# A transformer layer with window pooling on one core: sums in tiles of their own, pieces and high parts at other steps, a layer norm without GpSimd

## The chip, the core and the metric

The kernel runs on one core of a Trainium2 chip. A core has five engines with a queue each, worked off in program order: TensorE (PE, matrix products into PSUM banks of 128 x 512 floats), VectorE (DVE), ScalarE (ACT), GpSimd (POOL) and SyncE (SP, which here issues most transfers). They meet only at semaphores. The metric is the time of one execution on the device in microseconds (us).

## The reference

One layer for 1024 tokens of width 1024: a multi-scale pooling mixer, a layer norm, a SwiGLU channel mixer with hidden width 2816, and a second layer norm.

```python
x = layer_norm(ALPHA * x + g1 * ox, ln_g[i, 0], ln_b[i, 0])
x = layer_norm(ALPHA * x + g2 * swiglu(x * (1.0 + sc2) + sh2, ffn_w_in[i], ffn_w_out[i]),
               ln_g[i, 1], ln_b[i, 1])

def layer_norm(x, g, b):
    mu = jnp.mean(x, axis=-1, keepdims=True)
    var = jnp.mean(jnp.square(x - mu), axis=-1, keepdims=True)
    return (x - mu) * lax.rsqrt(var + LN_EPS) * g + b

def swiglu(h, w_in, w_out):
    gt, up = jnp.split(h @ w_in, 2, axis=-1)
    return (jax.nn.silu(gt) * up) @ w_out
```

## The kernel before

**Number format.** Every float32 operand of a product is split into a high part (a cast by ScalarE, `take_hi`, L267) and a low part (the rest, a subtraction by VectorE, `take_lo`, L270). A product is three matmuls: high x high, high x low, low x high.

**Fewer products.** Both matrix products of the channel mixer use a scheme of Strassen's kind: seven products of sums of blocks in place of eight products of blocks. The sums of the hidden activations a are made by VectorE (`a_sums`, `a_more_sums`) and stored in DRAM as a11, a2, s21 and s43. The sums of the output weights go to four DRAM tiles e1 to e4 and are made by 27 transfers that accumulate, the weight-sum pieces (`e_piece`, issued from GpSimd's queue); 18 of them stand in the loop over hidden blocks, nine in the last part.

**Three parts.** First come the modulation vectors, the pooling and the first layer norm; from 98 to 227 us the gate products; from 227 to 531 us the loop `period(f)` over 22 hidden blocks of 128. The last part, which the change is mostly about, is the output product: seven passes (`sub_pass(0)` to `sub_pass(6)`), one for each of the products p1 to p7, over 11 pairs of hidden blocks. A pair in a pass is a **step**; there are 77, numbered 0 to 76, 11 for each pass. One step is 12 matmuls: four row groups of 128 tokens, three matmuls each, into four banks. `heads` and `tails` group the first and last steps of a pass row group by row group, so that the row groups of a pass end apart; with `tails` 6 the last six steps are taken together.

**Order of the last part.** The Python code emits instructions in the order in which the engines' queues hold them. Ahead of each step `run_ahead` emits what is due: loads of step operands (`yraw`, two 128 x 512 transfers on SP's queue), splits (`yhi` by ScalarE, `ylo` by VectorE), pieces, and then the jobs that were given a time in steps: residual rows (`yrow`), products by the gate vector g2 (`scaled`), sums and the layer norm's steps. `LEAD` is how many steps the splits run ahead, growing over the passes, and `LOADS` how many more the loads do. Tiles of 128 x 1024 floats ("big") come from 45 places that are reused, the longest free first.

**Names.** u0 to u3, c0 to c3 and yv0, yv1 (two halves each) hold partial results of four row groups; `ps_x`, `ps_x2`, `ps_x3`, `ps_y`, `ps_y2` are the bank groups of the passes; mw holds a row's statistics. Rows 1 to 4 are finished in passes 5 and 6, rows 5, 6, 7 and 0 after pass 6. The mean and variance of a row come from `bn_stats` and `bn_aggr` on VectorE; for rows 5 to 0 the scaling is shared between ScalarE (`row_norm`), VectorE (`row_centre`, `row_scale`) and GpSimd (`by_line`).

Of the kernel before, what the change touches and what calls it, by code (L numbers as in the profile page):

```python
# [17 lines left out]
P = 128  # L18
# [201 lines left out]
def trunk_kernel(ctx: ExitStack, tc: tile.TileContext, x, c, mod_w, mod_b, ln_g, ln_b, ffn_w_in, ffn_w_out,  # L220
# [716 lines left out]
    def a_sums(j):  # L937

        x, y = tiles["a", 2 * j], tiles["a", 2 * j + 1]
        nc.vector.tensor_tensor(x[:, 1], y[:, 1], x[:, 1], ALU.subtract)  # L940
        nc.vector.scalar_tensor_tensor(x[:, 0], x[:, 1], -1.0, x[:, 0], ALU.mult, ALU.subtract)
        nc.sync.dma_start(s21_of[j], x)

    def a_more_sums(j):

        x, y = tiles["a", 2 * j], tiles["a", 2 * j + 1]
        for n in range(2):
            nc.vector.scalar_tensor_tensor(y[:, n], y[:, n], -1.0, x[:, 0], ALU.mult, ALU.subtract)

    def a_more_out(j):  # L950
        nc.sync.dma_start(s43_of[j], tiles["a", 2 * j + 1])
        done_with("big", f"a_{2 * j}", f"a_{2 * j + 1}")
# [101 lines left out]
    done = {"load": 0, "split": 0, "piece": IN_LOOP}  # L1054
# [6 lines left out]
    def step_split(n):  # L1061
        hi, lo = (big(f"y{q}{n}", F32R, (P, 2, HALF)) for q in ("hi", "lo"))
        split(hi, lo, raw.pop(n))
        operands[n] = hi, lo
        done_with("big", f"yraw{n}")

    def advance(kind, upto):
        while done[kind] < min(upto, STEPS):
            {"load": step_load, "split": step_split}[kind](done[kind])
# [61 lines left out]
    def row_stats(i, n, s):  # L1131
        if i not in st_of:
            st_of[i] = small(f"su{i}", (P, 3, 6), 8, "st")
        nc.vector.bn_stats(st_of[i][:, n, :], res[i][:, s])  # L1134

    def row_spread(i):
        mv = spread_of[i] = small(f"mw{i}", (P, 6), 8, "mv2")
        nc.vector.bn_aggr(mv[:, 0:2], st_of[i][:, : 3 if i == ORDER[1][3] else 2])

    def row_root(i):  # L1140
        mv = spread_of[i]
        nc.scalar.activation(mv[:, 2:3], mv[:, 1:2], ACT.Sqrt, bias=eps[:, 0:1])

    def row_factor(i):
        mv = spread_of[i]
        nc.vector.reciprocal(mv[:, 3:4], mv[:, 2:3])
        nc.vector.scalar_tensor_tensor(mv[:, 4:5], mv[:, 0:1], -1.0, mv[:, 3:4], ALU.mult, ALU.mult)

    def row_norm(i, s):
        mv, z = spread_of[i], res[i]  # L1150
        nc.scalar.activation(z[:, s], z[:, s], ACT.Identity, bias=mv[:, 4:5], scale=mv[:, 3:4])  # L1151

    def row_centre(i, s):
        z = res[i][:, s]
        nc.vector.scalar_tensor_tensor(z, z, spread_of[i][:, 0:1], lines["lg2"][:, s], ALU.subtract, ALU.mult)  # L1155

    def row_scale(i, s):
        z = res[i][:, s]
        nc.vector.scalar_tensor_tensor(z, z, spread_of[i][:, 3:4], lines["lb2"][:, s], ALU.mult, ALU.add)
# [5 lines left out]
    LEAD, LOADS = (3, 9), 4  # L1165
# [14 lines left out]
    def take_from(i, s, src):  # L1180
        z = res[i][:, s]
        nc.vector.tensor_tensor(z, z, src, ALU.subtract)
# [68 lines left out]
    with tc.manual_schedule():  # L1251
# [6 lines left out]
        advance("split", 3)  # L1258
# [22 lines left out]
        jobs = residual_jobs(0, 2.6, 2.2)  # L1281
# [6 lines left out]
        more = residual_jobs(1, 1.5 * PAIRS, 2.9)  # L1288
# [5 lines left out]
        jobs = [(1 + r, lambda r=r, i=i: add_into(i, first, c[r])) for r, i in enumerate(ORDER[0])]  # L1294
# [4 lines left out]
        jobs = [(r, lambda r=r, i=i: row_stats(i, 0, first)) for r, i in enumerate(ORDER[0])]  # L1299
        jobs += [(4, lambda: line_load("lg2", ln_g[1])), (4, lambda: line_load("lb2", ln_b[1]))]  # L1300
        more = [(t - PAIRS, job) for t, job in more if t >= PAIRS]
        for r, ps, _ in sub_pass(3, x_banks, True, 0, TAILS, jobs + more):
            v[r] = yv[r // 2][:, r % 2]
            nc.vector.tensor_tensor(v[r], ps, u[r], ALU.add)
        more = [(t - PAIRS, job) for t, job in more if t >= PAIRS]
        for r, ps, _ in sub_pass(4, x_banks, False, HEADS, TAILS, more):
            nc.vector.tensor_tensor(c[r], ps, u[r], ALU.add)
        y_banks = four("y2", "y")
        jobs, more = [], []
        for r, i in enumerate(ORDER[0]):  # L1310
            jobs.append((r / 2, lambda r=r: scaled(c[r], c[r], second)))
            jobs.append((r / 2 + 1, lambda r=r, i=i: take_from(i, second, c[r])))
            jobs.append((r / 2 + 2, lambda i=i: (row_stats(i, 1, second), row_spread(i))))
            jobs.append((r / 2 + 3, lambda i=i: row_root(i)))
            jobs.append((r / 2 + 4, lambda i=i: row_factor(i)))
            jobs.append((2 * r + 5, lambda i=i: row_centre(i, whole)))
            jobs.append((2 * r + 6, lambda i=i: row_scale(i, whole)))
            jobs.append((2 * r + 7, lambda i=i: row_out(i, whole)))
        more = [(t - PAIRS, f) for t, f in jobs if t >= PAIRS]
        for r, ps, _ in sub_pass(5, y_banks, True, 0, 1, jobs):  # L1320
            nc.vector.tensor_tensor(u[r], ps, u[r], ALU.add)
            nc.vector.tensor_tensor(v[r], ps, v[r], ALU.add)
        for r, i in enumerate(ORDER[1]):
# [50 lines left out]
```

## Time and profile before

| | |
|---|---|
| three timed runs | 764.58, 767.73, 768.26 us; median 767.73 |
| the profiled execution | 769.0 us, its span 767.2 us |
| VectorE busy | 565.1 us (74%) |
| ScalarE busy | 269.0 us (35%) |
| GpSimd busy | 172.2 us (22%) |
| transfers | 191.51 MB, mean 250 GB/s |

The span runs from the first to the last instruction of the profiled execution; what lies around it is 1.8 us. A row of a timeline has the start and the duration in us, the engine, the line, the operation, output <- inputs and a count; in brackets stands how long the engine was idle before and what released it. A row of the list of waits has the total in us, how many waits, and the longest. A row of the stages has the stretch, its length, the busy time of PE, PEld (weight loads), DVE, ACT and POOL with counts, the granted TensorE clock, the share of the DMA engines and GB/s. Back-to-back instructions of one engine overlap a little, so the distance of their starts is what one costs.

### The profile page before, as it was taken

How to read it: one execution, taken by the hardware profiler on the slowest of the kernel's cores; microseconds unless marked ns; L12 is line 12 of the kernel's file. 1: busy time of each engine (PE TensorE's matmuls, PEld its weight loads, DVE VectorE, ACT ScalarE, POOL GpSimd, SP SyncE). 2: the span in 40 equal slices, each digit the busy share in tenths (PEclk: the TensorE clock that was granted, in tenths of full speed). 3: DMA queues.
4: the chain of work that ended last, by engine and by line, in shares of the span. 5: the costliest groups of instructions: out<-in, count | busy, mean ns of one | idle time of the engine just before them, and what ended most of it. 6: DMA issues, size and time to landing. Idle time of an engine off the chain costs nothing.

```text
span 767.2 us, 9177 instructions
## 1 busy us (share of the span) xinstructions
PE 728.0 (95%) x3359; PEld 607.0 (79%) x3359; DVE 565.1 (74%) x686; ACT 269.0 (35%) x342; POOL 172.2 (22%) x132
## 2 busy tenths in 40 slices
PE   5988999999999999999999999998899999999991
PEld 5767988888887888888888888886678888888881
DVE  3598855517298787989889967864588759649997
ACT  0212873445982313113131131211467423334101
POOL 0000000020207554733725653511000000000015
PEclk8578999999999999999999999999999999999996
DMA  8998249585839698899999799699999858565202
GB/s 293 342 409 302 111 157 377 208 256 163 307 108 293 190 300 298 241 286 247 289 289 325 200 267 278 230 264 278 338 397 389 282 204 263 194 201 165 109 28 110
DMA packets 118019, 191.51 MB, mean 250 GB/s; under 512 B 7659, under 2 KB 66739, under 8 KB 117462
## 3 DMA queue, kind: packets, MB, share of 16 engines
q1 hardware_dynamic: 108326, 164.97, 62.5%
q0 software_dynamic: 9648, 25.95, 15.7%
q8 instruction: 26, 0.43, 0.2%
q14 instruction: 19, 0.16, 0.1%
HBM read 150.79 MB, written 66.06 MB: 283 GB/s over the span
## 4 chain that ended last, share of the span: by engine, by line
PE 74%; DVE 12%; DMA 10%; issue 2%; ACT 1%; POOL 0%; SPq 0%; POOLq 0%; DVEq 0%; ACTq 0%
PE ps_v L895 35%; PE ps_gate L761 15%; PE ps_x L1095 12%; DMA yraw<-in_ffn_w_out 5%; PE ps_y L1095 4%; DMA s21d<-a 2%; DMA mw<-in_mod_w 2%; PE ps_col L506 2%; DVE acc L491 2%; DVE ylo L270 2%; PE ps_pt L461 1%; DVE yrow L1155 1%; DVE su L1134 1%; PE ps_ox L262 1%; DVE yrow L1178 1%
## 5 line engine op out<-in xcount | busy, mean ns | idle before, releaser
L267 ACT CAST yhi<-yraw 128x1024 fp32r<-128x1024 f32 x77 | 79.6, 1053 | 88.6 <-PE ps_x L1095 21.5
L895 PE MATMUL ps_v<-t,w0h 128*128 128x512 f32 x352 | 109.3, 391 | 0.0
L761 PE MATMUL ps_gate<-h,wih 128*128 128x512 f32 x352 | 109.1, 391 | 0.0
L958 POOL TENSOR_TENSOR s<-raw,raw 128x512 f32<-128x512 f32 x22 | 30.9, 1405 | 323.6 <-DMA raw<-in_ffn_w_in 295.6
L270 DVE TENSOR_TENSOR ylo<-yraw,yhi 128x1024 fp32r<-128x1024 f32 x77 | 91.6, 1219 | 11.5 <-ACT yhi L267 8.2
L918 ACT ACTIVATE a<-a 128x512 f32<-128x512 f32 x22 | 13.9, 632 | 236.2 <-DVE a L917 236.2
L1095 PE MATMUL ps_x<-ylo,yhi 128*128 128x512 f32 (+1 forms) x231 | 88.6, 384 | 5.7 <-DVE ylo L270 5.7
L1095 PE MATMUL ps_x<-yhi 128*128 128x512 f32 (+1 forms) x231 | 88.4, 382 | 1.1 <-ACT u L1286 1.1
L1095 PE MATMUL ps_x<-yhi,ylo 128*128 128x512 f32 (+1 forms) x231 | 88.2, 382 | 0.0
L895 PEld LDWEIGHTS ps_v<-t,w0h 128*128 128x128 f32 x352 | 66.1, 188 | 14.5 <-issue 1.0
L761 PEld LDWEIGHTS ps_gate<-h,wih 128*128 128x128 f32 x352 | 65.7, 188 | 13.7 <-issue 0.5
L491 DVE SCALAR_TENSOR_TENSOR acc<-mw,s_col,acc 128x1024 f32<-128x1024 f32 x42 | 54.9, 1307 | 23.6 <-DMA mw<-in_mod_w 23.0
L895 PE MATMUL ps_v<-t,w0l 128*128 128x512 f32 x176 | 68.6, 390 | 1.8 <-DVE w0l L270 1.8
L761 PE MATMUL ps_gate<-h,wil 128*128 128x512 f32 x176 | 68.5, 389 | 0.0
L895 PE MATMUL ps_v<-t,ws 128*128 128x512 f32 x264 | 63.4, 389 | 0.0
L895 PEld LDWEIGHTS ps_v<-t,ws 128*128 128x128 f32 x264 | 49.6, 188 | 10.3
L1095 PEld LDWEIGHTS ps_x<-ylo,yhi 128*128 128x128 f32 x231 | 43.8, 190 | 15.7 <-DVE ylo L270 7.5
L1117 POOL TENSOR_TENSOR yrow<-yrow,line_lg 128x512 f32<-128x512 f32 (+2 forms) x4 | 5.8, 1460 | 224.0 <-ACT yrow L1151 224.0
L895 PE MATMUL ps_v<-h,w1h 128*128 128x512 f32 x176 | 54.2, 389 | 0.0
L895 PE MATMUL ps_v<-t,w1h 128*128 128x512 f32 x176 | 54.2, 389 | 0.0
L1095 PEld LDWEIGHTS ps_x<-yhi 128*128 128x128 f32 x231 | 43.8, 190 | 9.9 <-ACT u L1286 1.5
L1095 PEld LDWEIGHTS ps_x<-yhi,ylo 128*128 128x128 f32 x231 | 43.7, 189 | 8.1
(151 smaller groups left out, 1389.1 us busy)
## 6 DMA issues: line engine op xcount, KB each, us to landing
mw<-in_mod_w SPq DMA_DIRECT2D x48, 512.0 KB, 9.4
raw<-in_ffn_w_in SPq DMA_DIRECT2D x88, 256.0 KB, 6.6
ed<-in_ffn_w_out POOLq DMA_DIRECT2D x14, 1024.0 KB, 11.9
wi<-in_ffn_w_in SPq DMA_DIRECT2D x22, 512.0 KB, 6.0
yraw<-ed SPq DMA_DIRECT2D x44, 256.0 KB, 4.0
yraw<-in_ffn_w_out SPq DMA_DIRECT2D x33, 256.0 KB, 6.0
pd<-pk SPq DMA_DIRECT2D x11, 512.0 KB, 5.4
gd<-gk SPq DMA_DIRECT2D x11, 512.0 KB, 2.8
```

The source lines that it names most:

```text
L262: nc.tensor.matmul(ps, lh, rh, start=first, stop=False)
L267: nc.scalar.copy(hi, src)
L270: nc.vector.tensor_tensor(lo, src, hi.bitcast(F32), ALU.subtract)
L461: nc.tensor.matmul(pt_bank[half, ct][:, a:b], xr[ORDER[half][n]][:, ct * P : (ct + 1) * P], operand, start=n == 0, stop=False, skip_group_ ...
L491: nc.vector.scalar_tensor_tensor(acc, w, s_col[:, k : k + 1], acc, ALU.mult, ALU.add)
L506: nc.tensor.matmul(tiles["ps_col", j][:, n * WIDE : (n + 1) * WIDE], t[:, n * P : (n + 1) * P], by, start=first and n == 0, stop=last and ...
L761: nc.tensor.matmul(ps, x, y, start=k == n == 0, stop=k % 4 == 3 and n == 2, skip_group_check=k > 3)
L895: nc.tensor.matmul(ps, x, y, start=fresh and first, stop=last, skip_group_check=not fresh)
L918: nc.scalar.activation(a[:, 1], a[:, 1], ACT.Silu)
L958: nc.gpsimd.tensor_tensor(s, up1, up2, ALU.add)
L1095: nc.tensor.matmul(ps, s[x][:, r * P : (r + 1) * P], t[y][:, d], start=fresh and j == m == 0, stop=j == PAIRS - 1 and m == 2, skip_group_c ...
L1134: nc.vector.bn_stats(st_of[i][:, n, :], res[i][:, s])
```

## The change

**Sums.** `a_sums` and `a_more_sums` no longer overwrite the activations a; s21 and s43 get tiles of their own, and the activations' tiles come free earlier.

```diff
         x, y = tiles["a", 2 * j], tiles["a", 2 * j + 1]
-        nc.vector.tensor_tensor(x[:, 1], y[:, 1], x[:, 1], ALU.subtract)
-        nc.vector.scalar_tensor_tensor(x[:, 0], x[:, 1], -1.0, x[:, 0], ALU.mult, ALU.subtract)
-        nc.sync.dma_start(s21_of[j], x)
+        t = tiles["s21", j] = act_tile(f"s21_{j}")
+        nc.vector.tensor_tensor(t[:, 1], y[:, 1], x[:, 1], ALU.subtract)
+        nc.vector.scalar_tensor_tensor(t[:, 0], t[:, 1], -1.0, x[:, 0], ALU.mult, ALU.subtract)
+        nc.sync.dma_start(s21_of[j], t)
+        done_with("big", f"a_{2 * j}")
...
-        x, y = tiles["a", 2 * j], tiles["a", 2 * j + 1]
+        y, t = tiles["a", 2 * j + 1], act_tile(f"s43_{j}")
         for n in range(2):
-            nc.vector.scalar_tensor_tensor(y[:, n], y[:, n], -1.0, x[:, 0], ALU.mult, ALU.subtract)
+            nc.vector.scalar_tensor_tensor(t[:, n], y[:, n], -1.0, tiles["s21", j][:, 0], ALU.mult, ALU.subtract)
```

**Steps.** High and low parts are issued apart, the high part one step sooner; the lead grows to 11 steps, loads run three ahead of it; the nine last pieces get later step numbers.

```diff
         advance("load", int(step + ahead) + LOADS)
-        advance("split", int(step + ahead))
-        while done["piece"] < 3 * len(E_STEPS) and step >= 5 + 4.5 * (done["piece"] - IN_LOOP):
+        advance("hi", int(step + ahead) + 1)
+        advance("lo", int(step + ahead))
+        while done["piece"] < 3 * len(E_STEPS) and step >= 20 + 3 * (done["piece"] - IN_LOOP):
...
-    LEAD, LOADS = (3, 9), 4
+    LEAD, LOADS = (3, 11), 3
...
-        jobs = residual_jobs(0, 2.6, 2.2)
+        jobs = residual_jobs(0, 5, 2)
...
-        more = residual_jobs(1, 1.5 * PAIRS, 2.9)
+        more = residual_jobs(1, PAIRS, 2.1)
```

On SP's queue this moves the residual rows among the loads of pass 0. From the store of the last a11 on, before and after (xn is the stored residual row, `ffn_w_out` the output weights; yraw7 is the load of step 7):

```order
L933 DMA a11d10_86<-a_20_4098 128x512
L1059 DMA yraw7_4178<-a11d7_83 128x512
L1059 DMA yraw7_4178<-in_ffn_w_out 128x512
L1111 DMA yrow1_4185<-xn1_671 128x1024
L935 DMA a2d10_97<-a_21_4156 128x1024
L1059 DMA yraw8_4190<-a11d8_84 128x512
L1059 DMA yraw8_4190<-in_ffn_w_out 128x512
L942 DMA s21d10_108<-a_20_4098 128x1024
```

```order
L933 DMA a11d10_86<-a_20_4117 128x512
L1119 DMA yrow1_4204<-xn1_671 128x1024
L935 DMA a2d10_97<-a_21_4176 128x1024
L1063 DMA yraw7_4209<-a11d7_83 128x512
L1063 DMA yraw7_4209<-in_ffn_w_out 128x512
L943 DMA s21d10_108<-s21_10_4216 128x1024
L1063 DMA yraw8_4244<-a11d8_84 128x512
L1063 DMA yraw8_4244<-in_ffn_w_out 128x512
```

The first residual row and the store of a2 now pass ahead of step 7's loads; of the later residual rows the second moves from ahead of step 10 to behind it, and the third from ahead of step 14 to behind step 15. On ScalarE's queue, at the end of pass 0, where four copies take pass 0's result out of its banks into u0 to u3:

```order
L267 CAST yhi14_4387<-yraw14_4329 128x1024
L1286 COPY u0_4399<-ps_x_0_4174 128x512
L1286 COPY u1_4407<-ps_x_1_4175 128x512
L1286 COPY u2_4415<-ps_x_2_4176 128x512
L1286 COPY u3_4423<-ps_x_3_4177 128x512
L267 CAST yhi15_4428<-yraw15_4349 128x1024
```

```order
L267 CAST yhi14_4397<-yraw14_4353 128x1024
L267 CAST yhi15_4405<-yraw15_4373 128x1024
L1310 COPY u0_4415<-ps_x_0_4194 128x512
L1310 COPY u1_4423<-ps_x_1_4195 128x512
L1310 COPY u2_4431<-ps_x_2_4196 128x512
L1310 COPY u3_4439<-ps_x_3_4197 128x512
```

The high part of step 15 moved ahead of the copies. GpSimd's queue holds the nine pieces behind the sums of the last hidden block in both kernels, in the same order, and nothing between them.

**Banks.** Pass 6 (p7) goes on adding into the banks of pass 5 (p4), so that the sum of both comes out of one bank; it is taken row group by row group through all 11 steps, with four whole banks (before, the last row group was two halves). So the adds of pass 5's result into u, and u's product by g2, are gone from the end: u's own share of rows 5 to 0 is added in pass 3.

```diff
-        for r, ps, _ in sub_pass(5, y_banks, True, 0, 1, jobs):
-            nc.vector.tensor_tensor(u[r], ps, u[r], ALU.add)
+        for r, ps, _ in sub_pass(5, y_banks, True, 0, TAILS, jobs):
             nc.vector.tensor_tensor(v[r], ps, v[r], ALU.add)
...
-        for r, ps, d in sub_pass(6, x_banks, True, 0, 6, more):
+        for r, ps, d in sub_pass(6, y_banks, False, 0, PAIRS, more):
```

**Layer norm.** A row's sum comes from the accumulator outputs of the additions (`add_into`), its spread from a Square with accumulator on ScalarE; all rows but the last are then scaled by VectorE alone, one row behind. The last row keeps `bn_stats` and its division among three engines.

```diff
-    def row_spread(i):
-        mv = spread_of[i] = small(f"mw{i}", (P, 6), 8, "mv2")
-        nc.vector.bn_aggr(mv[:, 0:2], st_of[i][:, : 3 if i == ORDER[1][3] else 2])
+    def row_mean(i):
+        mv = row_sums(i)
+        nc.vector.tensor_scalar(mv[:, 2:3], mv[:, 0:1], mv[:, 1:2], -1.0 / D, ALU.add, ALU.mult)
+
+    def row_spread(i):
+        mv = row_sums(i)
+        nc.scalar.activation(scratch[0], res[i], ACT.Square, bias=mv[:, 2:3], accum_out=mv[:, 3:4])
+        nc.scalar.activation(mv[:, 4:5], mv[:, 3:4], ACT.Sqrt, bias=eps[:, 0:1], scale=1.0 / D)
...
-    def add_into(i, s, src):
+    def add_into(i, s, src, sign=1.0, sums=None):
         z = res[i][:, s]
-        nc.vector.tensor_tensor(z, z, src, ALU.add)
+        nc.vector.scalar_tensor_tensor(z, src, sign, z, ALU.mult, ALU.add,
+                                       **({} if sums is None else {"accum_out": row_sums(i)[:, sums : sums + 1]}))
...
+        def end_of_row(i):
+            row_factor(i)
+            row_centre(i, whole)
+            row_scale(i, whole)
+            row_out(i, whole)
```

On VectorE's queue, around the end of pass 5 (yv0 and yv1 take the result of pass 5 from the banks `ps_y2`; line_lg2 and line_lb2 are the norm's gain and shift), before and after:

```order
L270 TENSOR_TENSOR ylo74_5600<-yraw74_5520,yhi74_5599 128x1024
L1159 SCALAR_TENSOR_TENSOR yrow3_4315<-yrow3_4315,mw3_5453,line_lb2_5003 128x1024
L1321 TENSOR_TENSOR u0_4399<-ps_y2_0_5369,u0_4399 128x512
L1322 TENSOR_TENSOR yv0_4896<-ps_y2_0_5369,yv0_4896 128x512
L1321 TENSOR_TENSOR u1_4407<-ps_y2_1_5370,u1_4407 128x512
L1322 TENSOR_TENSOR yv0_4896<-ps_y2_1_5370,yv0_4896 128x512
L1321 TENSOR_TENSOR u2_4415<-ps_y2_2_5371,u2_4415 128x512
```

```order
L270 TENSOR_TENSOR ylo74_5596<-yraw74_5533,yhi74_5577 128x1024
L270 TENSOR_TENSOR ylo75_5613<-yraw75_5553,yhi75_5594 128x1024
L1160 SCALAR_TENSOR_TENSOR yrow3_4380<-yrow3_4380,mw3_4760,line_lg2_5120 128x1024
L270 TENSOR_TENSOR ylo76_5616<-yraw76_5574,yhi76_5611 128x1024
L1164 SCALAR_TENSOR_TENSOR yrow3_4380<-yrow3_4380,mw3_4760,line_lb2_5122 128x1024
L1348 TENSOR_TENSOR yv0_4934<-ps_y2_0_5408,yv0_4934 128x512
L1348 TENSOR_TENSOR yv0_4934<-ps_y2_1_5409,yv0_4934 128x512
```

The adds into u are gone, and the low parts of the last two steps and the third row's scaling now stand ahead of the first read of bank `ps_y2_0`.

More of the change, by code (lines that the diff above doesn't have):

```diff
@@ L1144, in row_factor, with row_sums @@
-    def row_factor(i):
[L1145 to L1151, printed above, removed]
+    def row_sums(i):
+        if i not in spread_of:
+            spread_of[i] = small(f"mw{i}", (P, 8), 8, "mv2")
+        return spread_of[i]
@@ L1328, in trunk_kernel @@
[L1328 to L1334 removed]
+            more.append((r, lambda r=r: scaled(v[r], v[r], second)))
```

130 lines of the change are left out of this document (72 added, 58 removed).

## The prediction

> **What bounds the kernel now.** I read the busy times first, then TensorE's waits, then the three engines round them in the last third.
>
> ```profile
> PE 728.0 (95%) x3359; PEld 607.0 (79%) x3359; DVE 565.1 (74%) x686; ACT 269.0 (35%) x342; POOL 172.2 (22%) x132
> PE ps_x L1095 <- DVE ylo L270: 5.7, 2, 3.3
> PE ps_x L1095 <- ACT u L1286: 1.1, 1, 1.1
> 600.50 29.92 PE ps_y L1095 x132
> 630.42 59.85 PE ps_x L1095 x264
> ```
>
> TensorE is busy 95% of the span, and the change leaves its work as it is: seven passes of 132 matmuls, 29.92 us each (0.227 us a matmul). So only what TensorE waits for, and what follows its last matmul, can go. After 380 us the list of waits has 6.8 us, all in the first pass (steps 0 to 10) or at its end; the chain runs without a gap from 570.28 through passes 1 to 4.
>
> ```profile
> 530.81 0.39 PE L1095 MATMUL ps_x<-yhi 128*128 128x512 f32 x1
> 533.66 0.50 PE L1095 MATMUL ps_x<-ylo,yhi 128*128 128x512 f32 x1 [2.47 <-DVE ylo L270]
> ...
> 537.51 0.39 PE L1095 MATMUL ps_x<-ylo,yhi 128*128 128x512 f32 x1
> ...
> 552.50 0.50 PE L1095 MATMUL ps_x<-ylo,yhi 128*128 128x512 f32 x1 [3.25 <-DVE ylo L270]
> ...
> 720.02 0.39 PE L1095 MATMUL ps_x<-yhi 128*128 128x512 f32 x1
> ...
> 750.35 0.28 PE L1095 MATMUL ps_x<-yhi,ylo 128*128 128x256 f32 x1
> ```
>
> Pass 0 starts at 530.81 and takes until 570.28, 9.5 us more than its work. Pass 6 starts at 720.02; TensorE ends at 750.63, and the span ends 16.6 us later. These are the two places.
>
> **Sums in tiles of their own.** VectorE's timeline shows what stands ahead of the low parts that TensorE waited for.
>
> ```profile
> 531.18 1.29 DVE L948 SCALAR_TENSOR_TENSOR a<-a,a 128x512 f32<-128x512 f32 x2 [6.19 <-DMA a2d<-a]
> 532.39 3.49 DVE L270 TENSOR_TENSOR ylo<-yraw,yhi 128x1024 fp32r<-128x1024 f32 x3
> ...
> 550.62 0.69 DVE L941 SCALAR_TENSOR_TENSOR a<-a 128x512 f32<-128x512 f32 x1 [4.99 <-DMA a11d<-a]
> 551.23 1.22 DVE L270 TENSOR_TENSOR ylo<-yraw,yhi 128x1024 fp32r<-128x1024 f32 x1
> ```
>
> Both sums overwrite a tile that is still being stored, and the low parts queue behind them. With other tiles both waits go. The arithmetic is the same, so the instructions cost what they cost. But what is late next? The loads:
>
> ```profile
> 500.00:545.00 45.00, 42.53 (x180) 34.44 (x179) 24.78 (x33) 9.56 (x11) 4.97 (x5) 0.96 1.09 265
> 545.00:600.00 55.00, 50.63 (x221) 40.99 (x220) 39.22 (x38) 32.06 (x33) 0.00 (x0) 1.00 1.05 392
> 546.60 1.05 ACT L267 CAST yhi<-yraw 128x1024 fp32r<-128x1024 f32 x1 [3.23 <-DMA yraw<-in_ffn_w_out]
> 548.83 1.05 ACT L267 CAST yhi<-yraw 128x1024 fp32r<-128x1024 f32 x1 [1.17 <-DMA yraw<-in_ffn_w_out]
> ...
> 568.70 1.05 ACT L267 CAST yhi<-yraw 128x1024 fp32r<-128x1024 f32 x1 [1.59 <-DMA yraw<-in_ffn_w_out]
> 569.65 2.04 ACT L1286 COPY u<-ps_x 128x512 f32<-128x512 f32 x4
> ```
>
> The last two columns of the stages are the DMA engines' share and GB/s: they are full from 500 to 600. ScalarE takes each high part when its load lands: step 5 at 546.60, step 6 at 548.83, step 14 at 568.70. A low part is ready 2.3 us after the landing (1.05 on ScalarE, 1.22 on VectorE). Without any wait TensorE would want step 5 at 530.81 + 5 x 2.72 = 544.4; it can have it at 548.9. So the first stall turns into waits for loads.
>
> From the landing of step 6 to that of step 14, 19.9 us, SP's queue has eight steps of two 128x512 loads (4 MB), three residual rows (1.5) and five stores (2.25): 7.75 MB, 0.39 MB/us. In its new order the first residual row and a store (1 MB) pass ahead of step 7, and the third residual row falls behind step 15. By bytes from 548.83, step 7 lands at 554.6, step 10 at 559.7, step 15 at 568.7 (again 7.75 MB). Step 10's low part, behind a residual row of 1.2 us on VectorE, is ready at 563.1. Steps 9 and 10 go together, 24 matmuls, and step 10 comes with the fourth: TensorE ends pass 0 at 563.1 - 0.9 + 5.4 = 567.6.
>
> **High parts a step sooner** adds nothing here, since high parts wait for landings; but it puts the high part of step 15 ahead of the four copies that free pass 0's banks. It is done at 568.7 + 1.05, the first copy about 0.5 later, and pass 1 starts at 570.3: as before. I take 0 for this place; bounds are a gain of 2.7 us (copies not held: 570.3 - 567.6) and, by TensorE's own rows, 7.5 us: the gaps of 2.47 and 3.25, and 1.8 for the slow clock behind the first (ten matmuls start from 533.66 to 537.51, nine steps of 0.43 instead of 0.227). A loss of 1.8 is possible too, if the clock falls in the same way behind the gap of 2.7 ahead of pass 1.
>
> The Trainium skill, "TensorE: Matmul & The Clock Gate", § Part 1: The HAM clock gate, lets the clock halve only after an idle window of about 3.4 us that runs free of the kernel. By it no gap here would be slowed and the sum stays at 0 for this place; by the rows behind 533.66 and 552.50, where 2.47 us were enough and 3.25 us were not, it can be 1.8 more.
>
> **Weight-sum pieces later.**
>
> ```profile
> 488.30 1.65 POOL L1043 DMA_DIRECT2D ed<-ed  x3
> ...
> 526.00 1.23 POOL L1043 DMA_DIRECT2D ed<-in_ffn_w_out  x1 [5.59 <-DMA ed<-in_ffn_w_out]
> ```
>
> The nine pieces of the loop over steps are all issued between 488 and 526, before step 0: they wait for each other and for nothing that TensorE does. GpSimd's queue has the same rows in the same order afterwards, so the later step number moves nothing: 0. If it did, pass 0's loads would have the 392 GB/s sooner.
>
> **Passes 1 to 4.** Products by g2 and sums move from pass 6 into pass 3, eight instructions of 0.6 us. VectorE has room:
>
> ```profile
> 600.00:690.00 90.00, 90.00 (x399) 74.55 (x398) 64.41 (x65) 33.23 (x32) 0.00 (x0) 1.00 0.68 220
> 690.00:720.00 30.00, 30.00 (x134) 24.84 (x133) 29.43 (x43) 13.42 (x16) 0.00 (x0) 1.00 0.47 158
> ```
>
> 4.8 us into 25.6 idle: 0.
>
> **Pass 5.** VectorE is full there (29.43 of 30). Now p7 is added into p4's banks, so pass 6's first matmul waits until VectorE has read bank 0 into yv0, and that read stands behind the low part of step 76 and the scaling of the third row.
>
> ```profile
> 690.30 0.69 DVE L1307 TENSOR_TENSOR c<-ps_x,u 128x512 f32<-128x512 f32 x1 [0.67 <-PE ps_x L1095]
> 690.90 1.22 DVE L270 TENSOR_TENSOR ylo<-yraw,yhi 128x1024 fp32r<-128x1024 f32 x1
> 692.04 1.29 DVE L1174 TENSOR_TENSOR c<-c,g 128x512 f32<-128x512 f32 x2
> 693.24 1.22 DVE L270 TENSOR_TENSOR ylo<-yraw,yhi 128x1024 fp32r<-128x1024 f32 x1
> 694.09 1.28 ACT L1142 ACT_TABLE_LOAD   x1
> 698.88 0.29 ACT L1142 ACTIVATE mw<-mw,eps 128x1 f32<-128x1 f32 x1 [3.51 <-DVE mw L1138]
> 706.35 1.28 DVE L1155 SCALAR_TENSOR_TENSOR yrow<-yrow,mw,line_lg 128x1024 f32<-128x1024 f32 x1
> L608 DVE DVE_READ_ACCUMULATOR x<-x,ps_ox x12: 80/83/84, 55.0 to 182.8; 128x1 f32 x12
> L629 ACT ACTIVATE sq<-x,mv x8: 1133/1136/1160, 79.8 to 194.6; 128x1024 f32<-128x1024 f32 x8
> L629 ACT ACTIVATION_READ_ACCUMULATOR sq<-x,mv x8: 183/186/194, 80.9 to 195.6; 128x1 f32 x8
> ```
>
> By the starts, a low part takes 1.14 us, half a row 0.60, a whole row 1.19; reading an accumulator 0.08. From 690.30: one sum 0.6, eleven low parts 12.5, four products 2.4, four sums with accumulator 2.7, six whole rows 7.1, eight small ones 0.8: 26.1. The bn_stats and bn_aggr of this stage are gone. ScalarE now does four squares (1.14, and 0.19 for the accumulator; the rows of the first layer norm's squares show both), four roots of 0.3 and the table load between high parts 68 and 70, so VectorE waits for two of them: high part 69 is done at about 701.5 and wanted at 699.9, high part 70 at 705.8 and wanted at 702.9, 4.5 us together (0.3 less where back-to-back instructions overlap). With 0.6 for yv0 itself it is read at 690.3 + 26.1 + 4.2 + 0.6 = 721.2, and TensorE could start at 720.02: a wait of **1.2**. Bounds: 0 (VectorE never waits) and 3 (each square waits for its own sum).
>
> All low parts are needed by 720 + 6.8, since pass 6 now takes row group 0 through all steps first; the last is done by about 719.4.
>
> **Pass 6 and the end.**
>
> ```profile
> 748.16 2.73 POOL L1117 TENSOR_TENSOR yrow<-yrow,line_lb 128x1024 f32<-128x1024 f32 x1
> ...
> 746.66 1.98 DVE L1155 SCALAR_TENSOR_TENSOR yrow<-yrow,mw,line_lg 128x512 f32<-128x512 f32 x1
> 748.74 2.17 DVE L1147 SCALAR_TENSOR_TENSOR mw<-mw 128x1 f32<-128x1 f32 x1
> ...
> 756.25 0.42 DVE L1174 TENSOR_TENSOR c<-ps_x,g 128x256 f32<-128x256 f32 x1
> ...
> 760.04 0.24 DVE L1138 BATCH_NORM_AGGREGATE mw<-su 128x2 f32<-128x18 f32 x1
> ```
>
> The last group is ready at 750.6, and VectorE comes to it at 756.25: the rows before it end within 8 us of each other, and GpSimd beside it stretches a 128x1 product to 2.17 us. Now groups end 7.48 us apart. VectorE's work for one (product, sum, mean, two whole rows: 3.8, and about 1.7 for ScalarE's square and root) fits, and what is left over from pass 5 ends by about 732, with the second group due at 736. So the last product starts with TensorE's end: 720.02 + 1.2 + 29.92 + 0.2 (the lag at 690.30) = 751.3. Product, sum, bn_stats: 2.2. bn_aggr starts at 753.5, not 760.04; from there on it is the same chain and a product of 0.1 more, so the span shrinks by **6.4** to 760.8. If yv0 costs nothing, 7.6; if it costs 3, 4.6.
>
> The profiled execution had 769.0 for its span of 767.2; it lies 1.3 over the median of 767.73. Taking 6.4 off the median gives **761.3 us**.
>
> **Rivals.**
> - *Pass 0 gains too.* For it: the waits name VectorE, whose waits go. Against it: full DMA engines and the landings above. 761.3 - 7.5 = 753.8; with half of it, 757.5. Chance 0.15.
> - *Pieces do move,* and pass 0's 9.5 us go: 751.8. GpSimd's rows speak against it. 0.02.
> - *More waits:* pass 1 starts with a slow clock (1.8) and yv0 costs 3: 761.3 + 1.8 + 1.8 = 764.9. 0.12.
> - *Slower than before:* ScalarE's squares hold high parts 69 to 76 and so VectorE and yv0; every us that yv0 is read after 721.2 is one of TensorE. It breaks even 6.4 later, at 727.6, and counts as slower from 10.3 later on. It needs VectorE to wait some 15 us in place of 4.2, when ScalarE has only 7 us of squares, roots and table load to put in the way; time 772. 0.04.
> - The forecast, 0.67.
>
> **How the numbers follow.** The forecast's own range is 759 to 763.5 (bounds of yv0, half a microsecond for the end). Half of the first rival and most of the third are taken in: 754.5 to 765. About 0.5% (3.8 us) is what a measurement can tell from no change: faster holds the forecast, the first two and a little of the third, 0.88; same 0.08; slower 0.04.
>
> **What would show it.** Right: no VectorE wait for a2d or a11d; ScalarE's high parts of pass 0 still behind yraw; pass 1 starting near 570; a wait of ps_y for yv0 of 0 to 3 us; 9 to 10 us between the last matmul and the end. Wrong: pass 1 starting before 567, or high parts 69 and 70 later than 708.

## The result, and the profile after

Six runs of the changed kernel took 760.29 to 765.08 us, median 761.82; six of the kernel before beside them 764.58 to 769.32, median 767.84. The ratio is 0.9939, 95% interval 0.9911 to 0.9967: the changed kernel is faster, by 6.0 us between the medians and by 2.5 to 6.8 us by the interval. The profiled execution is the longest of its six, 765.08 us with a span of 763.3.

The busy times on the page of the changed kernel:

```profile
PE 730.3 (96%) x3326; PEld 605.9 (79%) x3326; DVE 559.9 (73%) x675; ACT 275.0 (36%) x353; POOL 165.6 (22%) x126
```

and, from its list of waits, what TensorE waited for after 380 us (total, how many, longest):

```profile
PE ps_x L1103 <- DVE ylo L270: 3.3, 5, 0.8
PE ps_x L1103 <- ACT u L1310: 2.7, 1, 2.7
PE ps_x L1103 <- ACT yhi L267: 2.3, 2, 2.0
PE ps_y L1103 <- DVE yv L1348: 0.9, 1, 0.9
```

Before, two long waits for low parts stood here; now there are several short ones for low and high parts, one for the copies into u ahead of pass 1, and one for yv at the start of pass 6. The waits of pass 0 have not gone, they have changed their name. Rows of VectorE's and ScalarE's timelines of pass 0 say why:

```profile
544.14 0.69 DVE L941 TENSOR_TENSOR s<-a,a 128x512 f32<-128x512 f32 x1
...
550.40 1.23 DVE L270 TENSOR_TENSOR ylo<-yraw,yhi 128x1024 fp32r<-128x1024 f32 x1 [2.11 <-ACT yhi L267]
556.50 1.23 DVE L270 TENSOR_TENSOR ylo<-yraw,yhi 128x1024 fp32r<-128x1024 f32 x1 [4.87 <-ACT yhi L267]
555.42 1.04 ACT L267 CAST yhi<-yraw 128x1024 fp32r<-128x1024 f32 x1 [5.05 <-DMA yraw<-in_ffn_w_out]
```

The sums (L941) no longer wait for a store. The low parts now wait for their high parts, and these for their loads. The largest landing gap, 5.05 us, is step 7's, which stands behind a residual row and a store in the new order.

Rows of TensorE's and VectorE's timelines from the end of pass 5 to the end (c is the product of a row group of pass 6 by g2):

```profile
723.01 2.48 DVE L1348 TENSOR_TENSOR yv<-ps_y,yv 128x512 f32<-128x512 f32 x4
723.84 0.47 PE L1103 MATMUL ps_y<-yhi 128*128 128x512 f32 x1 [0.89 <-DVE yv L1348]
733.62 0.67 DVE L1200 TENSOR_TENSOR c<-ps_y,g 128x512 f32<-128x512 f32 x1
739.50 0.68 DVE L1200 TENSOR_TENSOR c<-ps_y,g 128x512 f32<-128x512 f32 x1
746.58 0.69 DVE L1200 TENSOR_TENSOR c<-ps_y,g 128x512 f32<-128x512 f32 x1 [1.11 <-PE ps_y L1103]
754.06 0.69 DVE L1200 TENSOR_TENSOR c<-ps_y,g 128x512 f32<-128x512 f32 x1 [1.50 <-PE ps_y L1103]
756.24 0.21 DVE L1174 BATCH_NORM_AGGREGATE mw<-su 128x2 f32<-128x12 f32 x1
```

The product of the last group waits for TensorE, with VectorE 1.50 us idle before it: VectorE has caught up by the third group (1.11 us idle). Before, VectorE came to the last group 5.6 us late. From pass 1's first matmul (573.04, where before it was 570.28) to bn_aggr are 183.20 us, where before it was 189.76.

### The profile page after: what moved, and what is told of

Its sections match the earlier page's. It is cut to its first block, busy times and chain, and to the rows that moved or that the text cites. A ratio compares the mean times of both kernels' runs of the same rounds, so it can differ in the third digit from the quotient of the medians.

```text
span 763.3 us, 9102 instructions
## 1 busy us (share of the span) xinstructions
PE 730.3 (96%) x3326; PEld 605.9 (79%) x3326; DVE 559.9 (73%) x675; ACT 275.0 (36%) x353; POOL 165.6 (22%) x126
## 4 chain that ended last, share of the span: by engine, by line
PE 65%; issue 16%; DMA 11%; DVE 5%; ACT 2%; POOL 0%; SPq 0%; POOLq 0%; DVEq 0%; ACTq 0%
PE ps_v L895 33%; PE ps_gate L761 13%; PE ps_x L1103 7%; DMA yraw<-in_ffn_w_out 4%; PE ps_y L1103 4%; DMA line_lb<-in_ln_b 3%; PE ps_col L506 2%; DVE acc L491 2%; PE ps_pt L461 1%; DMA a11d<-a 1%; PE ps_ox L262 1%; PE ps_ox L264 1%; PE ps_ox L263 1%; DMA x<-in_x 1%; DVE t L270 1%
## 5 line engine op out<-in xcount | busy, mean ns | idle before, releaser
L962 POOL TENSOR_TENSOR s<-raw,raw 128x512 f32<-128x512 f32 x22 | 33.1, 1504 | 320.4 <-DMA raw<-in_ffn_w_in 312.0
L1103 PE MATMUL ps_x<-yhi 128*128 128x512 f32 x176 | 69.6, 395 | 5.1 <-ACT u L1310 2.7
L1103 PE MATMUL ps_x<-ylo,yhi 128*128 128x512 f32 x176 | 69.8, 397 | 3.3 <-DVE ylo L270 3.3
L1103 PE MATMUL ps_x<-yhi,ylo 128*128 128x512 f32 x176 | 69.2, 393 | 0.0
L1103 PE MATMUL ps_y<-yhi 128*128 128x512 f32 x132 | 51.4, 390 | 0.9 <-DVE yv L1348 0.9
L1103 PE MATMUL ps_y<-ylo,yhi 128*128 128x512 f32 x132 | 51.4, 389 | 0.0
L1103 PE MATMUL ps_y<-yhi,ylo 128*128 128x512 f32 x132 | 51.3, 389 | 0.0
```

The costliest lines, as they stand in the source:

```text
L962: nc.gpsimd.tensor_tensor(s, up1, up2, ALU.add)
L1103: nc.tensor.matmul(ps, s[x][:, r * P : (r + 1) * P], t[y][:, d], start=fresh and j == m == 0, stop=j == PAIRS - 1 and m == 2, skip_group_c ...
```

## The experiments

Theory: the end gains, because VectorE is no longer behind at the last row group; pass 0 gains nothing, because its loads come late. The runs undo or do one part at a time, and some move the pieces as well. In the table, "pass 0" runs from its first matmul to pass 1's, "rest" from there to bn_aggr, both from the one profiled execution (the two runs with early pieces and the third row later have no gap between passes 0 and 1, so only the sum is given). Ratios are to the runs of the kernel before that stood beside each, whose medians lie between 766.90 and 767.86.

| run | median us | ratio (95%) | pass 0 | rest |
|---|---|---|---|---|
| before | 767.84 | | 39.47 | 189.76 |
| changed | 761.82 | 0.9939 (0.9911 to 0.9967) | 42.77 | 183.20 |
| sums alone | 766.61 | 0.9999 (0.998 to 1.0018) | 40.13 | 189.60 |
| end alone | 767.81 | 1.0013 (0.9992 to 1.0033) | 42.78 | 188.32 |
| steps alone | 766.63 | 1.0002 (0.9979 to 1.0025) | 42.18 | 189.28 |
| nine pieces early | 754.80 | 0.9842 (0.9784 to 0.99) | 30.66 | 183.19 |
| high parts not sooner | 765.20 | 0.9969 (0.9945 to 0.9993) | 39.13 | 188.85 |
| third row later | 761.20 | 0.993 (0.9903 to 0.9957) | 39.89 | 183.69 |
| shared norm | 761.66 | 0.9933 (0.9911 to 0.9955) | 41.72 | 183.20 |
| six steps | 766.75 | 1.0002 (0.9983 to 1.0022) | 41.40 | 188.59 |
| five early, third row later | 747.84 | 0.9736 (0.9698 to 0.9774) | 211.81 in all | |
| nine early, third row later | 752.84 | 0.9803 (0.9756 to 0.9851) | 211.92 in all | |
| groups alone | 766.24 | 0.9986 (0.9961 to 1.0012) | 39.78 | 189.81 |
| old sums | 761.10 | 0.9904 (0.9874 to 0.9934) | 41.89 | 183.20 |

How much one profile of pass 0 is worth can be read in the table: four kernels with the changed pass 0 word for word (changed, third row later, shared norm, six steps) lie between 39.89 and 42.77 there, and three with that of before (before, groups alone, end alone) between 39.47 and 42.78. The rest repeats far better: 183.20, 183.20, 183.20, 183.19, and 189.76, 189.60, 189.81.

### The sums alone

To the kernel before, only the first diff of the change (tiles of their own) is applied.

> The kernel before with the sums s21 and s43 in tiles of their own and nothing else of the change. Theory (the loads are late next): VectorE's waits of 6.19 and 4.99 us for the stores go, TensorE's waits in pass 0 turn into waits for low parts whose high parts wait for landings of yraw, pass 1 starts between 567.6 and 572 (before 570.28), time 0 to 2 us below the kernel before. Rival (VectorE's waits set pass 0): pass 1 starts near 563, 7.5 us less, time about 760.

Median 766.61, ratio 0.9999. VectorE's waits for stores are gone. Two rows of its timeline, the longest waits in pass 0, are a low part and a residual row:

```profile
535.90 1.23 DVE L270 TENSOR_TENSOR ylo<-yraw,yhi 128x1024 fp32r<-128x1024 f32 x1 [5.77 <-ACT yhi L267]
...
549.59 1.22 DVE L1121 TENSOR_TENSOR yrow<-yrow,line_lg 128x1024 f32<-128x1024 f32 x1 [4.04 <-DMA yrow<-xn]
```

The rival (7.5 us) falls: pass 0 takes 40.13 us, where before it was 39.47, and pass 1 starts at 568.16. The waits that went were covered by others that came due at the same time: ScalarE's high parts of steps 3 to 8 each wait 0.9 to 3.5 us for a load.

### The old sums in the changed kernel

```diff
-        t = tiles["s21", j] = act_tile(f"s21_{j}")
-        nc.vector.tensor_tensor(t[:, 1], y[:, 1], x[:, 1], ALU.subtract)
...
+        nc.vector.tensor_tensor(x[:, 1], y[:, 1], x[:, 1], ALU.subtract)
...
```

and so on: the inverse of the first diff, with all else of the change kept.

> The changed kernel with the sums s21 and s43 written over the activations again, as before. Theory (the sums' own tiles neither gain nor cost anything, in company as alone): VectorE's waits for the stores are back in pass 0 and TensorE's waits with them, pass 1 starts between 567 and 573 as in the other runs, from pass 1's start to bn_aggr 183.2 us, time within 1.5 us of the changed kernel's 761.8. Rival (the new order of residual rows and stores needs the own tiles): a wait of over 5 us in pass 0, pass 1 starts after 573, time 764 to 768.

Median 761.10, the rest 183.20. VectorE's waits for the two stores are back (5.38 and 6.17 us), and pass 0 takes 41.89 us, within what the changed pass 0 takes without them. In company as alone, the sums' own tiles are worth nothing that can be measured.

### The steps alone

To the kernel before, the second diff of the change is applied (high parts sooner, lead, loads, residual rows, pieces).

> The kernel before with high parts a step sooner, lead 11 and loads 3 ahead, the residual rows' and the pieces' new step numbers, and nothing else. Theory of the prediction: no change, pass 1 starts at 570.3 within 1, time within 1 us of before. Rival (what the profile of the changed kernel shows is the steps' doing): the copies behind the high part of step 15 and a load of steps 7 and 15 that lands 1 to 3 us later put pass 1 at 572 to 573.5, time 1.5 to 3 us above before.

Median 766.63, ratio 1.0002: no change. But not because nothing happened. In this profile pass 0 took 2.7 us longer than in that of before (no more than the scatter of pass 0), pass 1 began with a slow clock, and the end came sooner. The chain of waits (start, length, what):

```profile
568.38 31.86 PE ps_x L1099 x132
600.24 29.92 PE ps_y L1099 x132
```

A pass is 29.92 us; this one took 31.86, behind a gap of 1.96 us. From pass 1's start to bn_aggr are 189.28 us, of which about 1.7 (31.86 less the 30.21 of pass 1 in other runs) are the clock's; without it the end of the kernel before would be 2.1 us shorter with these steps. The gain at the end stands out, since the rest without these steps repeats within 0.3 us; that the slow clock and pass 0 take it up again is read from this one profile.

### The end alone

The changed kernel with the sums, the order of steps, the lead and the first residual rows of before; the second half's residual rows stay as in the change.

> The changed kernel with the sums, the steps' order, the lead and the first residual rows of before, so that the banks and the layer norm are changed alone. Theory: pass 1 starts as before (570 within 1), from pass 6's first matmul to the end 39.5 us in place of 47.2, a wait of 0.5 to 3 us ahead of pass 6, time 4.5 to 7.5 us below the kernel before, near 761.5. Rival (the end's gain needs the longer lead, since the high parts of steps 69 and 70 stand behind ScalarE's squares): the wait ahead of pass 6 is over 4 us, time above 764.

Median 767.81, ratio 1.0013: the theory is wrong for this run, and the rival (the wait ahead of pass 6 over 4 us, time above 764) is right. Rows of VectorE's and TensorE's timelines at the end of pass 5:

```profile
704.18 1.23 DVE L270 TENSOR_TENSOR ylo<-yraw,yhi 128x1024 fp32r<-128x1024 f32 x1 [3.98 <-ACT yhi L267]
710.32 1.22 DVE L270 TENSOR_TENSOR ylo<-yraw,yhi 128x1024 fp32r<-128x1024 f32 x1 [3.19 <-ACT yhi L267]
727.65 0.68 PE L1095 MATMUL ps_y<-yhi 128*128 128x512 f32 x1 [4.41 <-DVE yv L1339]
728.13 0.63 PE L1095 MATMUL ps_y<-ylo,yhi 128*128 128x512 f32 x1
```

The same two low parts in the changed kernel:

```profile
703.89 1.23 DVE L270 TENSOR_TENSOR ylo<-yraw,yhi 128x1024 fp32r<-128x1024 f32 x1 [1.14 <-ACT yhi L267]
707.76 1.22 DVE L270 TENSOR_TENSOR ylo<-yraw,yhi 128x1024 fp32r<-128x1024 f32 x1 [2.51 <-ACT yhi L267]
```

VectorE waits 7.2 us for high parts behind ScalarE's squares, where in the changed kernel it waits 3.65. It reads yv0 so much later, and TensorE waits 4.41 us at the start of pass 6 and then starts with a slow clock (0.63 us a matmul in place of 0.39). The end behind it works as in the changed kernel: the last product finds VectorE idle for 1.50 us.

### High parts not a step sooner

```diff
-        advance("hi", int(step + ahead) + 1)
+        advance("hi", int(step + ahead))
```

> The changed kernel with high parts issued together with the low parts of their step again (lead 11 and all else as in the change). Theory (the sooner high part pays in pass 5 and costs in pass 0): the copies of pass 0's result stand ahead of the high part of step 15 and pass 1 starts 0.5 to 2.7 us after pass 0's last matmul less than in the changed kernel; in pass 5 VectorE waits about 7 us for high parts 69 and 70 in place of 3.65, the wait ahead of pass 6 grows from 0.9 to 3.5 to 4.5 us and the clock falls behind it (1.6 us), so from pass 1's start to bn_aggr 187 to 188.5 us in place of 183.2; time 763 to 767. Rival (lead 11 alone is what pass 5 needs): 183 to 184 us, time 759 to 762.

Median 765.20: 3.4 above the changed kernel, with everything else of the change in place. VectorE waits 3.98 and 3.19 us for the two high parts, as in the end alone, and TensorE's wait is back:

```profile
702.70 1.23 DVE L270 TENSOR_TENSOR ylo<-yraw,yhi 128x1024 fp32r<-128x1024 f32 x1 [3.19 <-ACT yhi L267]
719.22 2.47 DVE L1348 TENSOR_TENSOR yv<-ps_y,yv 128x512 f32<-128x512 f32 x4
720.04 0.76 PE L1103 MATMUL ps_y<-yhi 128*128 128x512 f32 x1 [4.40 <-DVE yv L1348]
```

So the lead of 11 alone doesn't let pass 5 carry the squares; the high part a step sooner does it. Whether it would do so without the lead of 11 was not run. The part of the theory on pass 0 isn't borne out: the copies stand ahead of high part 15 here, and pass 1 still waits 2.57 us for them, since they stand behind high part 14, which waits for its load as well.

### The last six steps

```diff
-        for r, ps, d in sub_pass(6, y_banks, False, 0, PAIRS, more):
+        for r, ps, d in sub_pass(6, y_banks, False, 0, 6, more):
```

> The changed kernel with the last six steps of pass 6 taken row group by row group as before, so that the groups end 4.08 us apart in place of 7.48. Theory (the order of row groups pays): VectorE's 3.8 us a row and its waits for ScalarE's square and root (1.7) don't fit in 4.08, the last product starts 1 to 4 us after TensorE's end, time 1 to 4 us above the changed kernel. Rival (what pays is u's work gone and GpSimd left out): last product within 0.5 us of TensorE's end, no change.

Median 766.75, ratio 1.0002: this one number gives the whole gain back, a little more than the theory's 1 to 4 us. VectorE's products of the four groups:

```profile
740.00 0.69 DVE L1200 TENSOR_TENSOR c<-ps_y,g 128x512 f32<-128x512 f32 x1 [8.11 <-PE ps_y L1103]
745.90 0.68 DVE L1200 TENSOR_TENSOR c<-ps_y,g 128x512 f32<-128x512 f32 x1
749.20 0.16 DVE L1156 RECIPROCAL mw<-mw 128x1 f32<-128x1 f32 x1 [1.64 <-ACT mw L1152]
751.78 0.68 DVE L1200 TENSOR_TENSOR c<-ps_y,g 128x512 f32<-128x512 f32 x1
...
757.67 0.68 DVE L1200 TENSOR_TENSOR c<-ps_y,g 128x512 f32<-128x512 f32 x1
```

VectorE is idle for 8.11 us and then gets four groups 4.08 us apart, while it needs 5.88 for each (745.90 to 751.78), 1.64 of them a wait for ScalarE's square and root. The last product starts 5.9 us behind TensorE's last matmul (which starts at 751.81). A row group's work must fit into the distance of the groups: 5.88 fits into 7.48, not into 4.08.

### The groups alone

The same number, changed in the kernel before (`sub_pass(6, x_banks, True, 0, PAIRS, more)`).

> The kernel before with one number changed: the last eleven steps of pass 6, not the last six, are taken row group by row group (7.48 us apart for the first three); banks, layer norm, sums and steps as before. Theory (the distance of the row groups is what pays, and GpSimd, u's adds and the separate banks are not): the last group's product starts within 1.5 us of TensorE's end in place of 5.6 late, time 4 to 6.5 us below before, 761.5 to 764. Rival (VectorE's work on u and GpSimd beside it are too much for any distance, so the banks are needed): last product 4 to 6 us late, no change.

Median 766.24, ratio 0.9986: no change, and the rival holds. Rows of VectorE's and TensorE's timelines:

```profile
716.54 0.68 DVE L1321 TENSOR_TENSOR u<-ps_y,u 128x512 f32<-128x512 f32 x1
...
738.01 0.66 DVE L1174 TENSOR_TENSOR c<-ps_x,g 128x512 f32<-128x512 f32 x1
...
755.33 0.41 DVE L1174 TENSOR_TENSOR c<-ps_x,g 128x256 f32<-128x256 f32 x1
726.13 0.50 PE L1095 MATMUL ps_x<-ylo,yhi 128*128 128x512 f32 x1 [2.16 <-DVE ylo L270]
...
751.11 0.28 PE L1095 MATMUL ps_x<-yhi,ylo 128*128 128x256 f32 x1
```

From 716.54 VectorE works without a wait, most of all on u and yv, and comes to the first group only at 738.01, after some 60% of pass 6. Its last product starts 4.2 us behind TensorE's last matmul, although TensorE itself is late here: in the new order it needs the last steps' low parts within the first row group, waits 2.16 us for one behind VectorE's work on u, and goes on with a slow clock. From the first add into u to bn_aggr VectorE needs 40.31 us here (716.54 to 756.85) and 40.27 in the kernel before, with one wait of 0.36 us in each: its own work sets the end of both. So the distance of the groups is not enough as long as VectorE has this work. Of it, some 4.9 us are four operations that are stretched beside GpSimd (1.98 us for 0.75, 2.17 for 0.16, 1.47 for 0.69, 1.44 for 0.59); whether the old banks with GpSimd left out would have gained was not run.

### The old division of the norm

Rows 5, 6 and 7 as before: bn_stats and bn_aggr, then

```diff
-            row_mean(i)
-            row_spread(i)
-            to_end.append(i)
+            last_spread(i)
...
+            last_factor(i)
+            last_norm(i, slow_part[r])
...
+            by_line(i, slow_part[r], "lg2", ALU.mult, nc.gpsimd)
+            by_line(i, slow_part[r], "lb2", ALU.add, nc.gpsimd)
```

> The changed kernel with rows 5, 6 and 7 normed as before (bn_stats and bn_aggr, ScalarE's scaling, GpSimd's two passes over the right half or the whole row), on the new banks and the new order of row groups. Theory (the row groups, 7.48 us apart, and u's work gone are what pays; GpSimd does its rows in the gaps): the last product starts within 1 us of TensorE's end, time within 1 us of the changed kernel. Rival (GpSimd beside VectorE is what held the end): VectorE's 2 us operations come back, the last product starts 2 to 5 us late, time 764 to 767.

Median 761.66, the rest 183.20. Two products and bn_aggr by VectorE's timeline:

```profile
742.42 0.69 DVE L1200 TENSOR_TENSOR c<-ps_y,g 128x512 f32<-128x512 f32 x1 [0.23 <-PE ps_y L1103]
749.90 0.69 DVE L1200 TENSOR_TENSOR c<-ps_y,g 128x512 f32<-128x512 f32 x1 [2.72 <-PE ps_y L1103]
752.08 0.21 DVE L1174 BATCH_NORM_AGGREGATE mw<-su 128x2 f32<-128x12 f32 x1
```

The last group finds VectorE idle for 2.72 us, more than the 1.50 of the changed kernel. Taking GpSimd out of these three rows, which stands in the title, is worth nothing once the rest of the change is there.

### The third row's scaling later

```diff
-            jobs.append((2.5 * r + 4, lambda i=i: row_centre(i, whole)))
...
+            t = 2.5 * r + (4 if r < 2 else 6)
+            jobs.append((t, lambda i=i: row_centre(i, whole)))
...
```

> The changed kernel with the scaling of the third and fourth row two steps later, so that the four reads into yv0 and yv1 stand ahead of it on VectorE. Theory: the wait of 0.9 us ahead of pass 6 goes, from pass 1's start to bn_aggr 182.0 to 182.4 us in place of 183.2, time 1 us below the changed kernel. Rival (the rows put off run into pass 6's groups): the groups' products start late, no gain or a loss of 1 to 2 us.

The wait ahead of pass 6 is gone from the list of waits. The rest is 183.69, but in this run a gap of 3.42 us ahead of pass 1 brought the slow clock (the pass takes 31.88 in place of 30.21); without it 182.02, 1.2 below the changed kernel. The median, 761.20, is 0.6 below, less than the measurement can tell.

### Nine pieces in the gate products

The functions `block` and `e_piece` move up unchanged; the gate products' stores issue nine pieces, and the loop goes on from there (t is the gate tile that is stored).

```diff
...
+        if name == "gk" and pair < EARLY:
+            nc.gpsimd.tensor_tensor(hold, t[:, 0, 0:1], t[:, 1, 0:1], ALU.add)
+            e_piece(pair)
...
-            e_piece(f - 1)
+            e_piece(EARLY + f - 1)
```

> The changed kernel with the first nine pieces issued during the gate products (98 to 227 us, where the DMA engines have a third of their time free), each behind a 128x1 sum on GpSimd that reads a gate tile; the loop then holds pieces 10 to 27, and none is left for after the loop. Theory (pass 0 waits because the DMA engines are full, the pieces among it): TensorE's waits in pass 0 shrink from about 10 us to 0 to 4, pass 1 starts 6 to 10 us sooner than in the changed kernel, time 752 to 756. Rival (eight transfers in flight or the stores of the activations set the landings, not bandwidth): landings and pass 1's start stay within 2 us, time 760 to 762.

Median 754.80, ratio 0.9842. In pass 0 TensorE waits for nothing; 0.58 us ahead of pass 1 is all that is left. Pass 0 takes 30.66 us in place of 42.77. But it starts at 538.16, 7.9 later than in the changed kernel, so pass 1 starts only 4.2 us sooner, not 6 to 10: the pieces now disturb the gate products. From the first of these to the loop's first matmul are 135.0 us in this profile (97.74 to 232.72), where in the changed kernel it was 129.7; the other run with nine early pieces has 132.2. Stages (stretch, length, busy times, clock, DMA share, GB/s) of the gate products and the loop's start, changed kernel first, then this one:

```profile
130.00:160.00 30.00, 30.00 (x142) 25.16 (x141) 12.96 (x17) 12.82 (x18) 0.00 (x0) 1.00 0.68 234
190.00:227.00 37.00, 37.00 (x182) 31.10 (x181) 19.51 (x24) 33.07 (x48) 5.18 (x4) 1.00 0.58 207
```

```profile
130.00:160.00 30.00, 28.43 (x133) 23.22 (x132) 14.10 (x18) 11.50 (x16) 1.90 (x4) 1.00 0.91 336
190.00:227.00 37.00, 34.67 (x167) 28.43 (x166) 16.37 (x26) 34.31 (x49) 10.28 (x10) 1.00 0.97 274
```

Of the four stretches of the gate products, TensorE's busy time (third figure) falls below the length in these two, where the DMA share is above 0.9; in the other two it is full, at shares of 0.72 and 0.79.

### Five or nine early, with the third row later

Five pieces behind every second pair of the gate products, then one in each of the 22 periods:

```diff
...
+        if name == "gk" and pair % 2 == 0 and pair < 2 * EARLY:
+            nc.gpsimd.tensor_tensor(hold, t[:, 0, 0:1], t[:, 1, 0:1], ALU.add)
+            e_piece(pair // 2)
...
-        if 0 < f <= IN_LOOP:
-            e_piece(f - 1)
+        e_piece(EARLY + f)
```

> The changed kernel with the third and fourth row's scaling two steps later and the pieces moved: five during the gate products (one behind every second pair), then one in each of the 22 periods of the loop. Theory (pass 0 waits for bandwidth; nine pieces in 130 us of gate products disturb the loads there, five do so less): pass 0 without waits or with less than 3 us, the loop's end within 4 us of the changed kernel's 530.3, time 748 to 753. Rival (the loop has no DMA time left, and its weights come late): TensorE waits in the loop, time 754 to 760.

> The changed kernel with the third and fourth row's scaling two steps later and the first nine pieces during the gate products, as in the run with nine. Theory (the two gains add): 1 us below the run with nine pieces alone, 753 to 755. Rival (the gain of one is taken up by the other's stage): no better than 754.8.

With nine, the median is 752.84, 2.0 below nine alone; with four runs each, which spread over 6.8 and 10.7 us, that the gains add isn't shown. With five it is 747.84, just below what was expected: 19.8 us below the runs of the kernel before beside it (767.67) and 14 below the changed one, the fastest version here. The gate products take 129.8 us in its profile, as without pieces. The chain of waits of the run with five:

```profile
527.70 59.84 PE ps_x L1110 x264
587.54 29.92 PE ps_y L1110 x132
```

From its view of the transfers between 490 and 600 us, the two queues and one kind of load:

```profile
q1 hardware_dynamic: 14843, 32.01, 78.9%
q0 software_dynamic: 744, 1.46, 7.2%
...
yraw<-a11d SPq DMA_DIRECT2D x11, 256.0 KB, 4.2
```

The same view of the changed kernel:

```profile
q1 hardware_dynamic: 12613, 27.44, 68.0%
q0 software_dynamic: 3344, 8.65, 36.3%
...
yraw<-a11d SPq DMA_DIRECT2D x11, 256.0 KB, 13.5
```

Passes 0 and 1 run as one piece of 59.84 us, twice 29.92. The columns of a queue are packets, MB and share of the engines; of an issue, count, size and median us to landing. The pieces (software queue) took 36.3% of the engines' time for 8.65 MB, the other transfers 68.0% for 27.44 MB. With the pieces gone, a load of a11 lands in 4.2 us after its issue in place of 13.5.

## Why the prediction was right, and where it was not

The time (761.3 against a median of 761.82) and most terms held. That they meet within half a microsecond is in part luck: pass 0 alone scatters by some 3 us between single profiles, and the interval of the ratio leaves 2.5 to 6.8 us for the gain.

- *Pass 0 gains nothing from the sums.* Right, and shown from both sides: sums alone 0.9999, old sums in the changed kernel 761.10.
- *The size of this term was 0, and no run tells another.* The four profiles with the changed pass 0 have a mean of 41.4 us, the three with that of before 40.7; the difference is inside their scatter. The landings behind the 0 were too early: step 7's high part was put at 554.6 and step 15's at 568.7, and they began at 555.42 and 571.46. The 7.75 MB that were counted from step 6's landing (here 549.32) to step 15's took 22.1 us, 0.35 MB/us and not 0.39. So pass 1 started at 573.04, 2.7 us later than the 570.3 of the prediction. The slow clock of the bound did come in this profile, but inside pass 0, behind gaps of 2.04 and 0.76 us.
- *Pieces later: nothing.* Right: the last piece is issued at 527.90, before step 0. The condition that it named ("if it did, pass 0's loads would have the 392 GB/s sooner") is shown by the runs with early pieces, and is worth more than all of the change.
- *Pass 5 and yv0: a wait of 1.2.* Measured 0.89 by the row, 1.06 by the start of pass 6. High parts 69 and 70 let VectorE wait 1.14 and 2.51 us, 3.65 in place of the 4.2 of the sum.
- *The end: 6.4 less.* From pass 1's start to bn_aggr 6.56 less (189.76 to 183.20). The medians differ by 6.0; what the stages ahead of pass 1 add or take is within the scatter of single profiles.
- *What the prediction didn't have:* that each of these parts is needed. It costed the high part a step sooner in pass 0 alone ("adds nothing here") and took the order of pass 5 as given; there it is worth 3.4 us by the medians. And it named GpSimd beside VectorE as one reason for the late last group; the shared norm shows that GpSimd does no harm once u's work is gone and the groups are 7.48 us apart. That GpSimd stretches VectorE's operations when they meet remains true: the 1.98 and 2.17 us rows are there again in the run with the groups alone.
- *The rival that was slower* had a mechanism that exists (ScalarE's squares hold the high parts, VectorE and yv0); the sooner high parts are what keeps it away. Without them it takes 3.5 us more of wait and a slow clock behind it, 5.65 us of the rest and 3.4 of the median. The 6.4 us at which the end would break even are not reached by this alone.

So the 6.0 us need three edits at once: u's work out of VectorE's queue by the shared banks, the row groups 7.48 us apart, and the high parts a step sooner, since the shared banks make pass 6 wait for VectorE. Two of the three are shown by taking them away. Take away the distance (six steps), and the time is that of before; take away the sooner high parts, and 3.4 us go, or all of it with the other steps and the sums gone too (end alone); the distance alone moves nothing. The banks weren't taken away by themselves: that they, and not a smaller edit beside them, are the third is argued from VectorE's 40.3 us in the run with the groups alone, and not shown by a run of its own.

## What to carry to other kernels

When an engine is late at the end, compare its time for one group with the distance at which the groups arrive: here 5.88 us fitted into 7.48 and not into 4.08, and with 4.08 the rest of the change gained nothing. An edit that measures as nothing alone can be needed by another: try it both ways, alone in the old kernel and taken away from the new one. And where transfers limit a stage, move those that nothing waits for to a stage with free transfer time, but thinly: nine pieces made the gate products 5.3 and 2.5 us longer in two profiles, five 0.1 us.

## What the runs showed of the hardware

The clock of TensorE after a gap did not follow the gap's length. Behind 1.96 us (steps alone) and 3.42 us (third row later) some eight matmuls ran at 0.43 us in place of 0.23, and the pass took 31.86 and 31.88 us; behind 2.16, 2.57 and 2.74 us (shared norm, high parts not sooner, changed kernel) it took 30.21 to 30.23. The gap of 2.16 us in pass 6 of the groups alone, as long as that of the shared norm, was followed by the slow clock. Every gap of 3.34 us or more between 520 us and the end of these profiles was. The slow stretch can begin after the gap has ended, as the matmuls of the run with the third row later show:

```profile
567.46 0.50 PE L1103 MATMUL ps_x<-yhi 128*128 128x512 f32 x1 [3.42 <-ACT u L1310]
...
568.51 0.40 PE L1103 MATMUL ps_x<-ylo,yhi 128*128 128x512 f32 x1
568.74 0.59 PE L1103 MATMUL ps_x<-yhi,ylo 128*128 128x512 f32 x1
569.13 0.63 PE L1103 MATMUL ps_x<-yhi 128*128 128x512 f32 x1
```

The Trainium skill, "TensorE: Matmul & The Clock Gate", § Part 1: The HAM clock gate, has the clock judged over a window of about 3.4 us that runs free of the kernel. That a gap of 2.16 us can pass or not agrees with a free window; that 1.96 us can be enough does not agree with a window that must be idle from end to end.

The pieces that accumulate cost more transfer time for a byte than those that copy. (Not all 27 pieces accumulate: the first three of each of the four sums are plain copies.) The software queue of the changed kernel from 230 to 300 us, where six pieces copy, and from 512 to 552 us, where its pieces accumulate:

```profile
q0 software_dynamic: 1500, 5.76, 24.4%
q0 software_dynamic: 2246, 4.44, 60.4%
```

24.4% of 70 us for 5.76 MB is 3.0 us of all the engines for each MB, 60.4% of 40 us for 4.44 MB is 5.4. The transfers of the other queue took 2.7 between 490 and 600 us (68.0% of 110 us for 27.44 MB).
